# A fused two-layer kernel on one core: the first two weight units of layer 1 are fetched together and run chunk by chunk

## The chip, the cores and the metric

One Trainium2 chip, one of its cores. The metric is the device time of one execution in microseconds (us); where several executions are given, it is their median. The engines are PE (TensorE, matmuls), DVE (VectorE), ACT (ScalarE), POOL (GpSimd) and SP (SyncE, which here only issues DMA). ACT and POOL issue DMAs of their own as well.

## What is computed

Two layers over 1024 latent tokens and 256 context tokens, model width 1024, batch 1, all in float32. Layer 0 mixes tokens by two chunkwise recurrences, layer 1 by windowed attention and by a diagonal state-space scan (S5). The reference, cut to the second layer:

```python
h = rmsnorm(x, norm_g[layer]) * (1 + scale) + shift          # for latents and for context
q, k, v, g_att, u, g_s5 = split_cols(h @ w_in, OD_SPLITS)    # widths 1024, 256, 256, 1024, 1024, 1024
att = window_attention(rope(q), rope(k), v, sink)            # 128-token band, all context keys, a sink
ssm = s5_bidirectional(u, ...)                               # 64 groups of 16 channels, 64 complex states each
z = gelu(ssm); a, b = split(z @ glu_w, 2); s5 = a * sigmoid(b)
y = concat([att * silu(g_att), s5 * silu(g_s5)]) @ w_out
out = rmsnorm(x + gate * y, final_norm_g)                    # latents only
```

## The kernel before

**Matmuls of float32 in three passes.** A weight unit is a tile of 128 x 1024: 128 output features by 8 blocks of 128 inputs. SP loads it (`wraw`, line 116, one buffer), ACT rounds it to its high part `whi` (line 64) and DVE subtracts to get the low part `wlo` (line 65). The token side is held the same way as `hh` and `hl`. `mm3` (lines 69 to 71) then runs three matmuls for each block: high by high, high by low, low by high. A chunk of tokens costs 8 x 3 = 24 matmuls into one PSUM tile named `mm`, of which there are two.

**Chunks.** The tokens lie in three chunks, `CHUNKS`: 256 context tokens (`hh0`, `hl0`), then 512 latents (`hh1`, `hl1`), then the last 512 (`hh2`, `hl2`). The normalised rows of the last chunk are the last thing that layer 0's output stage makes: PE transposes them (line 287), DVE scales them (`nt`, line 294), ACT and DVE split them into `hh2` and `hl2` (lines 64 and 65).

**Weight stream.** `Stream` hands units out in a fixed order. `get` cuts the next unit (splits it into `whi` and `wlo`) if that is not done yet and issues the next load; `ahead` cuts the unit after that while the current one runs. In layer 1 the even units among the first ten live in one pool, `pre`, and the odd ones in another, one buffer for each half. `g_fm` runs one unit over all its chunks: get, then for each chunk 24 matmuls, the evacuation, and `ahead(0)` after the first chunk.

**Layer 1** (`layer1`) weaves two threads in program order. `main()` runs the layer's products, called *layer matmuls* here: eight `u` units (evacuated by `ev_u` to `sg`, line 949, and sent to DRAM as `uF` from ACT's DMA queue, line 950), then `v`, two `k` units, and the units of gates and `q`. `side()` runs S5 on 32 pairs of channel groups, called *pairs 0 to 31*. For a pair, the *front* is a product on PE (`pd<-ut,bt`, line 1611), its copy on ACT (`sd`, lines 1615 to 1617), the scan with its multiplications on DVE (`rq` and `uw`, lines 1628 to 1638) and a copy on ACT (`sx`, lines 1640 and 1641). The *back* is products on PE into `yo` (line 1651 with `mt`, line 1653 with `sx`). For every second pair a set of matrices is built on PE, ACT, DVE and through small SP transfers (`s5kd`, `mt`, lines 1542 and 1545). Pair 4k needs the u units up to k, which `nu` counts.

**Order.** The kernel is built with a scheduler of the tile framework (`schedule_with_timeline_sim=True`): it takes the program order, the dependences and the buffers and fixes one order for every engine, which then runs in that order. So an edit at the start of layer 1 can change rows much later. Layer 0 and everything up to the transposes of the last chunk stand in the same order on PE in both kernels. After layer 1's weave, attention, the GLU products and the output products follow.

Of the kernel before, what the change touches and what calls it, by code (L numbers as in the profile page):

```python
# [54 lines left out]
class Body:  # L55
# [92 lines left out]
    def g_fm(self, st, hs, evac):  # L148

        (wh, wl), = st.get()  # L150
        for ci, (hh, hl, c0, n) in enumerate(hs):
            ps = self.bank("mm", 2)
            for ko in range(8):
                w = slice(ko * 128, ko * 128 + 128)
                self.mm3(ps[:, :n], wh[:, w], wl[:, w], hh[:, ko, :], hl[:, ko, :], ko == 0, ko == 7)
            evac(ps[:, :n], c0, n)
            if ci < st.hl_b - 1:
                st.ahead(ci)
            yield

    def g_tm(self, st, hs, evac):
# [742 lines left out]
    def layer1(self):  # L904
# [13 lines left out]
        st = self.st  # L918
# [9 lines left out]
        with tc.tile_pool(name="psum1", bufs=1, space=PSUM, reuse_waits="tile") as ps5:  # L928
            s5 = S5(self, ps5, uF, zF)
            nu = [0]  # L930
# [12 lines left out]
                    yield  # L943

            def main():
                for i in range(8):
                    def ev_u(ps, c0, n):
                        t = self.stg.tile([128, 512], F32, name="sg", tag="sg", bufs=2)[:, :n].rearrange("p (t n) -> p t n", t=8)
                        S.activation(t, ps.rearrange("p (n t) -> p t n", t=8), AF.Copy)
                        self.nc.scalar.dma_start(  # L950
                            uF[i * 8:i * 8 + 8, :, c0 // 8:(c0 + n) // 8].rearrange("g (h t) n -> (g h) t n", t=8), t)

                    yield from self.g_fm(st, self.hs, ev_u)
                    nu[0] += 1

                def ev_v(ps, b):
# [17 lines left out]
                for kind, i in oB:  # L974
                    def ev(ps, c0, n):
                        lc = slice(c0 - 256, c0 - 256 + n)
                        if kind == "q":
                            self.rope(ps, c0, n, 0.125, [
                                qD[lc.start // 128:lc.stop // 128, i // 2, a * 32:a * 32 + 32,
                                   i % 2 * 2 + h].rearrange("b d t -> d b t")  # L980
                                for a in range(2) for h in range(2)])
                        elif kind == "ga":
                            t = self.silu(ps, n)
                            self.nc.scalar.dma_start(gaD[i, :, lc], t)
                        else:
                            t = self.stg.tile([128, 8, 64], F32, name="sg", tag="sg", bufs=2)
                            S.activation(t, ps.rearrange("p (n t) -> p t n", t=8)[:, ::-1], AF.Silu)
                            self.nc.scalar.dma_start(gsD[i, :, :, lc.start // 8:lc.stop // 8], t)

                    yield from self.g_fm(st, self.hs[1:], ev)  # L990

            weave(main(), side(), 24 + 10 + 6 + 2 * len(oB) - 6, s5.steps + 9)
        self.right.close()
        if self.stop == "l1":
# [4 lines left out]
        with ExitStack() as low:  # L999
# [23 lines left out]

            att = self.g_att(ai, ap, pa, qD, kD, vD, gaD)
            main = main()
            advance(main)
            advance(att)
            weave(main, att, 46, 150)
# [774 lines left out]
```

## Time and profile before

| | us |
|---|---|
| median of 3 runs | 2721.9 (2720.25 to 2723.5) |
| the profiled execution | 2724.01 |
| its span in the trace | 2722.2 |
| layer 1's layer matmuls and S5, about | 1551 to 2150 |
| attention, GLU and output products | from about 2150 to the end |

The trace covers 2722.2 us of the profiled execution's 2724.01; the other 1.8 us lie around it, and its mean granted clock was 0.99. The profiled execution is 2.1 us above the median of the runs. All positions below are microseconds from the span's start. PE records of float32 products that are not split (those of S5) appear twice for each instruction, so that four products show as x8.

### The profile page before, as it was taken

The page shows a single profiled execution, that of the slowest core. Times are in us where ns is not written, and L with a number is a line of the kernel's source. Part 1 is how long each engine was busy: PE and PEld are TensorE (multiplying, and loading weights), DVE is VectorE, ACT ScalarE, POOL GpSimd, SP SyncE. Part 2 cuts the span into 40 slices and gives each one's busy share as a digit, 9 for nine tenths or more (in the row PEclk, how much of TensorE's full clock was granted, in tenths as well). Part 3 has the DMA queues.
Part 4 walks back from the last instruction along what each step waited for, and adds up shares of the span by engine and source line. Part 5 has one row for each costly group of instructions (what it writes and reads, how often), then busy time and mean ns, then how long its engine had stood idle before and what let it go on. Part 6 is the DMA issues. An engine that isn't in the chain of part 4 may idle for free. (4 is left out here: it accounts for less than half of the span.)

```text
span 2722.2 us, 44690 instructions
## 1 busy us (share of the span) xinstructions
PE 2636.9 (97%) x15680; PEld 2274.3 (84%) x15680; DVE 1861.4 (68%) x4794; ACT 1374.3 (50%) x2917; POOL 488.4 (18%) x881
## 2 busy tenths in 40 slices
PE   6999999999999999999999999899999999999998
PEld 3998989898798898888787788787888888888887
DVE  5556655464664565646657688899994488898896
ACT  5445545434545445436324324677775455576552
POOL 1121121212212222222100000010010022225520
PEclk9999999999999999999999999999999999999999
DMA  6001011111111111112454545345446523253333
GB/s 243 28 31 56 21 57 35 49 53 53 57 49 47 57 57 32 57 57 84 142 187 146 177 122 137 93 118 127 118 109 182 157 83 112 78 159 112 124 115 130
DMA packets 235520, 262.15 MB, mean 96 GB/s; under 512 B 87520, under 2 KB 179936, under 8 KB 235040
## 3 DMA queue, kind: packets, MB, share of 16 engines
q1 hardware_dynamic: 174528, 223.89, 26.9%
q10 hardware_dynamic: 55712, 20.46, 2.9%
q0 software_dynamic: 5056, 14.95, 1.8%
q8 instruction: 124, 2.03, 0.3%
q14 instruction: 100, 0.82, 0.1%
HBM read 192.69 MB, written 66.52 MB: 95 GB/s over the span
## 5 line engine op out<-in xcount | busy, mean ns | idle before, releaser
L69 PE MATMUL mm<-hh,whi 128*128 128x512 f32 (+1 forms) x1800 | 671.4, 373 | 15.3 <-ACT gt L583 5.1
L71 PE MATMUL mm<-hh,wlo 128*128 128x512 f32 (+1 forms) x1800 | 668.0, 372 | 0.9 <-DVE wlo L65 0.8
L70 PE MATMUL mm<-hl,whi 128*128 128x512 f32 (+1 forms) x1800 | 663.6, 369 | 0.5 <-DVE hl L65 0.5
L69 PEld LDWEIGHTS mm<-hh,whi 128*128 128x128 f32 x1800 | 340.9, 189 | 69.5 <-issue 6.6
L71 PEld LDWEIGHTS mm<-hh,wlo 128*128 128x128 f32 x1800 | 340.1, 189 | 55.6 <-issue 1.8
L70 PEld LDWEIGHTS mm<-hl,whi 128*128 128x128 f32 x1800 | 340.6, 189 | 52.9 <-DVE hl L65 1.2
L70 PE MATMUL mm<-owl,yh 128*128 128x512 f32 x576 | 226.2, 394 | 4.8 <-DVE owl L65 4.7
L69 PE MATMUL mm<-owh,yh 128*128 128x512 f32 x576 | 226.8, 395 | 1.4 <-ACT yh L64 1.4
L71 PE MATMUL mm<-owh,yl 128*128 128x512 f32 x576 | 226.3, 394 | 0.0
L65 DVE TENSOR_TENSOR wlo<-wraw,whi 128x1024 fp32r<-128x1024 f32 x117 | 145.3, 1242 | 95.7 <-ACT whi L64 95.3
L69 PE MATMUL mm<-whi,hh 128*128 128x256 f32 x720 | 205.7, 286 | 3.1 <-DVE v L364 3.1
L70 PE MATMUL mm<-wlo,hh 128*128 128x256 f32 x720 | 205.4, 285 | 0.0
L71 PE MATMUL mm<-whi,hl 128*128 128x256 f32 x720 | 202.5, 281 | 0.0
L64 ACT ACTIVATE whi<-wraw 128x1024 fp32r<-128x1024 f32 x117 | 123.6, 1056 | 125.7 <-PE mm L70 104.9
L563 DVE SCALAR_TENSOR_TENSOR S<-S,sc,st 128x128 f32<-128x128 f32 (+1 forms) x192 | 74.3, 387 | 161.8 <-PE st L558 161.3
L1155 ACT ACTIVATE P<-P,ast 128x640 f32<-128x640 f32 (+1 forms) x128 | 101.6, 796 | 99.8 <-DVE ast L1156 66.7
L1161 POOL TENSOR_TENSOR P<-P,ast 128x640 f32<-128x640 f32 (+1 forms) x64 | 87.1, 1361 | 342.5 <-DVE ast L1159 199.2
L69 PEld LDWEIGHTS mm<-whi,hh 128*128 128x128 f32 x720 | 135.6, 188 | 5.1 <-DVE v L364 4.1
L70 PEld LDWEIGHTS mm<-wlo,hh 128*128 128x128 f32 x720 | 136.0, 189 | 1.4 <-issue 0.2
L71 PEld LDWEIGHTS mm<-whi,hl 128*128 128x128 f32 x720 | 135.5, 188 | 0.6
L70 PEld LDWEIGHTS mm<-owl,yh 128*128 128x128 f32 x576 | 108.3, 188 | 28.2 <-DVE owl L65 7.2
L69 PEld LDWEIGHTS mm<-owh,yh 128*128 128x128 f32 x576 | 108.2, 188 | 26.2 <-ACT ot L870 3.4
(407 smaller groups left out, 6071.5 us busy)
## 6 DMA issues: line engine op xcount, KB each, us to landing
wraw<-in_w SPq DMA_DIRECT2D x117, 512.0 KB, 3.7
yr<-yT SPq DMA_DIRECT2D x144, 128.0 KB, 2.6
owr<-in_wo SPq DMA_DIRECT2D x62, 256.0 KB, 5.5
whi<-in_wada SPq DMA_DIRECT2D x24, 512.0 KB, 3.5
adaw<-in_adaw SPq DMA_DIRECT2D x16, 512.0 KB, 10.2
qr<-qD SPq DMA_DIRECT2D x64, 128.0 KB, 2.8
yT<-gt SPq DMA_DIRECT2D x28, 256.0 KB, 2.3
x1p<-xr SPq DMA_DIRECT2D x10, 512.0 KB, 3.5
```

Of the source, the lines that this page charges most:

```text
L64: self.S.activation(hi, src, AF.Copy)
L65: (eng or self.V).tensor_tensor(lo, src, hi.bitcast(F32), op=OP.subtract)
L69: T.matmul(ps, sh, mh, start=first, stop=False)
L70: T.matmul(ps, sh, ml, start=False, stop=False)
L71: T.matmul(ps, sl, mh, start=False, stop=last)
L563: V.scalar_tensor_tensor(new, state[d], scal(d, b, 6, 7), pst[:, :dv], op0=OP.mult, op1=OP.add)
L1155: S.activation(p[:, j, :w], p[:, j, :w], AF.Exp, bias=nm[:, j:j + 1], accum_out=sm[:, j:j + 1])
L1161: G.tensor_tensor(p[:, 1, :w], p[:, 1, :w], es[:, 1:2].to_broadcast([128, w]), op=OP.mult)
```

## The change

The generator `fm` is new: `g_fm` without its own `get` and `ahead`. The first two u units are taken by one `get(2)`. Four runs of `fm` follow: unit 0 over the chunks 0 and 1, unit 1 over the chunks 0 and 1, unit 0 over chunk 2, unit 1 over chunk 2. `ahead(0)`, which cuts unit 2, comes after unit 0's chunk 2, and each of the two units is counted in `nu` after its chunk 2. The six other u units go through `g_fm` as before. `ev_u` becomes a factory, so that it keeps the unit's number. Lines of the changed kernel are 9 higher from line 160 on and 20 higher behind this place.

```diff
--- before.py
+++ after.py
@@ -156,6 +156,15 @@
             evac(ps[:, :n], c0, n)
             if ci < st.hl_b - 1:
                 st.ahead(ci)
+            yield
+
+    def fm(self, wh, wl, hs, evac):
+        for hh, hl, c0, n in hs:
+            ps = self.bank("mm", 2)
+            for ko in range(8):
+                w = slice(ko * 128, ko * 128 + 128)
+                self.mm3(ps[:, :n], wh[:, w], wl[:, w], hh[:, ko, :], hl[:, ko, :], ko == 0, ko == 7)
+            evac(ps[:, :n], c0, n)
             yield
 
     def g_tm(self, st, hs, evac):
@@ -943,14 +952,25 @@
                     yield
 
             def main():
-                for i in range(8):
-                    def ev_u(ps, c0, n):
+                def ev_u(i):
+                    def ev(ps, c0, n):
                         t = self.stg.tile([128, 512], F32, name="sg", tag="sg", bufs=2)[:, :n].rearrange("p (t n) -> p t n", t=8)
                         S.activation(t, ps.rearrange("p (n t) -> p t n", t=8), AF.Copy)
                         self.nc.scalar.dma_start(
                             uF[i * 8:i * 8 + 8, :, c0 // 8:(c0 + n) // 8].rearrange("g (h t) n -> (g h) t n", t=8), t)
 
-                    yield from self.g_fm(st, self.hs, ev_u)
+                    return ev
+
+
+                us = st.get(2)
+                for k, hs in ((0, self.hs[:2]), (1, self.hs[:2]), (0, self.hs[2:]), (1, self.hs[2:])):
+                    yield from self.fm(*us[k], hs, ev_u(k))
+                    if hs[0] is self.hs[2]:
+                        nu[0] += 1
+                        if k == 0:
+                            st.ahead(0)
+                for i in range(2, 8):
+                    yield from self.g_fm(st, self.hs, ev_u(i))
                     nu[0] += 1
 
                 def ev_v(ps, b):
```

ACT at the start of layer 1, before, with what each row waits for. `nt` is the scaled last chunk, `sg` a unit's evacuation (`mm_16989` and `mm_17124` are unit 0's chunks 0 and 1), `whi_17017` unit 1's high part:

```order
L64 ACTIVATE hh2_15700<-nt_16958 128x2x256 [waits DVE_49]
L949 ACTIVATE sg_17014<-mm_16989 128x256 [waits DMAHW0_49,PE_49]
L64 ACTIVATE whi_17017<-wraw_16559 128x1024
L949 ACTIVATE sg_17149<-mm_17124 128x512 [waits DMAHW7_49,DMAHW1_49,PE_49]
L950 DMA uF_16970<-sg_17014 1024x1x32 [waits DMAHW4_49,Activation_49]
```

The same place after. Unit 1's high part is now `whi_16989`, unit 0's chunk 0 is `mm_16995`:

```order
L64 ACTIVATE hh2_15700<-nt_16958 128x2x256 [waits DVE_49]
L64 ACTIVATE whi_16989<-wraw_16559 128x1024
L958 ACTIVATE sg_17020<-mm_16995 128x256 [waits DMAHW0_49,PE_49]
L958 ACTIVATE sg_17149<-mm_17124 128x512 [waits DMAHW7_49,DMAHW1_49,PE_49]
L959 DMA uF_16970<-sg_17020 1024x1x32 [waits DMAHW6_49,Activation_49]
```

Unit 1's split changes places with the first evacuation, and both still stand behind the last split of `hh2`. On PE the products of unit 1 over chunks 0 and 1 stand behind the last transposes in the place where unit 0's chunk 2 stood.

PE in the S5 pairs, before: `yo_20010` and `yo_20160` are the back products of pairs 14 and 15, `sb` and `sk` build matrices, `pd` is a front product, and `mm_20678` and `mm_20715` are layer matmuls (the rows left out between two `mm` rows are of the same two tiles):

```order
L1653 MATMUL yo_20010<-sx_19670,ct_19565 128x128 x2
L70 MATMUL mm_20678<-hl2_15701,whi_20466 128x512
...
L1514 MATMUL sb_20043<-cst_63,G_20031 128x128 x4
L1520 MATMUL sk_20049<-G_20031,kc_20027 32x128 x8
L1611 MATMUL pd_20064<-ut_19913,bt_19705 128x160 x4
L1651 MATMUL yo_20160<-ut_19606,mt_19556 128x128
L71 MATMUL mm_20678<-hh2_15700,wlo_20467 128x512
...
L71 MATMUL mm_20715<-hh1_15698,wlo_20602 128x512
L1653 MATMUL yo_20160<-sx_19823,ct_19565 128x128 x2
```

The same place after, without a row left out:

```order
L1673 MATMUL yo_20010<-sx_19670,ct_19565 128x128 x2
L1671 MATMUL yo_20160<-ut_19606,mt_19556 128x128
L1534 MATMUL sb_20037<-cst_63,G_20031 128x128 x4
L1534 MATMUL sb_20043<-cst_63,G_20031 128x128 x4
L1540 MATMUL sk_20049<-G_20031,kc_20027 32x128 x8
L1631 MATMUL pd_19922<-ut_19913,bt_19705 128x160 x4
L1673 MATMUL yo_20160<-sx_19823,ct_19565 128x128 x2
L1671 MATMUL yo_20160<-ut_19606,mt_19556 128x128
L1673 MATMUL yo_20160<-sx_19823,ct_19565 128x128 x2
L1544 MATMUL sk_20049<-cst_63,kq_20058 128x128
L69 MATMUL mm_20430<-hh1_15698,whi_20315 128x512
```

After pair 12's back products no layer matmul stands on PE until behind pair 15's; the next one is `mm_20430`, whose weights are the unit `whi_20315`.

SP at the load of that unit, `wraw_20158`, before (`bq`, `kc`, `dd` are constants of S5, `s5kd` and `mt` the small transfers of its matrices, `ut` reads `uF`):

```order
L116 DMA wraw_20008<-in_w1 128x1024
L1542 DMA s5kd_70<-kfb_19132 16x4x16 x8
L1545 DMA mt_19250<-s5kd_70 16x4x128 x8
L1504 DMA kc_20027<-in_s5kc 128x256
L116 DMA wraw_20158<-in_w1 128x1024
```

And after:

```order
L1562 DMA s5kd_70<-kfb_19730 16x4x16 x8
L1624 DMA ut_19913<-uF_16970 16x4x160 x2
L1565 DMA mt_19864<-s5kd_70 16x4x128 x8
L1624 DMA ut_19913<-uF_16970 16x4x160
L116 DMA wraw_20158<-in_w1 128x1024
```

The load moved behind the transfers of two further sets of matrices (`mt_19556` and `mt_19864`).

## Rows read from the trace of the kernel before

**Rows 1.** The page's busy times.

```profile
PE 2636.9 (97%) x15680; PEld 2274.3 (84%) x15680; DVE 1861.4 (68%) x4794; ACT 1374.3 (50%) x2917; POOL 488.4 (18%) x881
```

**Rows 2.** Timeline, PE, start of layer 1: start, us, engine, line, tiles, idle before.

```profile
1562.65 0.63 PE L287 MATMUL o<-cst,xn 128*128 128x128 f32 x4 [0.86 <-DVE nt L294]
1563.56 0.63 PE L287 MATMUL o<-cst,xn 128*128 128x128 f32 x4 [0.28 <-DVE nt L294]
1567.80 0.79 PE L69 MATMUL mm<-hh,whi 128*128 128x512 f32 x1 [3.62 <-ACT sg L949]
...
1571.38 0.63 PE L71 MATMUL mm<-hh,wlo 128*128 128x512 f32 x1
1571.81 0.57 PE L69 MATMUL mm<-hh,whi 128*128 128x512 f32 x1
...
1572.45 0.40 PE L71 MATMUL mm<-hh,wlo 128*128 128x512 f32 x1
1572.68 0.39 PE L69 MATMUL mm<-hh,whi 128*128 128x512 f32 x1
```

**Rows 3.** Busy by stretch, PE alone: length, busy (records), PEclk, DMA share, GB/s.

```profile
1567.80:1571.80 4.00, 4.00 (x9) 0.50 0.50 95
```

**Rows 4.** Timeline, ACT, the same place.

```profile
1566.85 0.63 ACT L64 ACTIVATE hh<-nt 128x512 fp32r<-128x512 f32 x1 [1.07 <-DVE nt L294]
1567.38 0.37 ACT L949 ACTIVATE sg<-mm 128x256 f32<-128x256 f32 x1
1567.65 1.05 ACT L64 ACTIVATE whi<-wraw 128x1024 fp32r<-128x1024 f32 x1
1568.60 0.58 ACT L949 ACTIVATE sg<-mm 128x512 f32<-128x512 f32 x1
```

**Rows 5.** Waits of PE, 1740 to 1910: us in total, times, longest.

```profile
PE yo L1653 <- ACT sx L1641: 9.8, 3, 8.5
```

**Rows 6.** Timeline, PE: front of pair 4, backs of pairs 4, 12 and 15.

```profile
1731.46 1.25 PE L1611 MATMUL pd<-ut,bt 128*128 128x160 f32 x8
1732.55 0.33 PE L1537 MATMUL sk<-kfb,shift 128*128 128x64 f32 x2
...
1744.63 1.22 PE L1653 MATMUL yo<-sx,ct 128*128 128x128 f32 x4 [8.53 <-ACT sx L1641]
...
1844.28 0.61 PE L1653 MATMUL yo<-sx,ct 128*128 128x128 f32 x4
...
1879.67 0.61 PE L1653 MATMUL yo<-sx,ct 128*128 128x128 f32 x4
```

**Rows 7.** Timeline, ACT: the last copy before pair 15's back.

```profile
1875.32 0.63 ACT L1641 ACTIVATE sx<-uw 64x512 f32<-64x512 f32 x1
```

**Rows 8.** Timeline, DVE, behind it: a low part and a rotary step.

```profile
1878.73 1.22 DVE L65 TENSOR_TENSOR wlo<-wraw,whi 128x1024 fp32r<-128x1024 f32 x1 [0.29 <-ACT whi L64]
1879.87 1.48 DVE L1632 TENSOR_TENSOR_SCAN rq<-dec,sd 128x640 f32<-128x640 f32 x1
...
1889.01 0.69 DVE L897 TENSOR_TENSOR rp<-mm,rot 128x512 f32<-128x512 f32 x1 [1.26 <-ACT rp L895]
1889.62 0.68 DVE L898 TENSOR_TENSOR rp<-rp,rot 128x512 f32<-128x512 f32 x1
```

**Rows 9.** Busy by stretch: length, PE, PEld, DVE, ACT, POOL (records), PEclk, DMA.

```profile
1844.30:1879.70 35.40, 31.84 (x198) 26.65 (x197) 35.01 (x49) 24.94 (x50) 0.00 (x0) 0.95 0.47 118
1879.70:2068.30 188.60, 187.19 (x1064) 157.94 (x1063) 178.50 (x249) 137.24 (x249) 16.67 (x32) 1.00 0.48 118
2068.30:2300.00 231.70, 231.70 (x1247) 199.92 (x1246) 148.62 (x383) 117.33 (x231) 34.78 (x35) 1.00 0.47 136
```

**Rows 10.** The same view, attention and output stages to the end.

```profile
2300.00:2450.00 150.00, 145.96 (x868) 127.80 (x867) 130.06 (x385) 94.21 (x222) 33.72 (x28) 0.98 0.38 118
2450.00:2600.00 150.00, 147.45 (x881) 129.80 (x880) 130.79 (x360) 91.79 (x230) 76.01 (x59) 1.00 0.40 126
2600.00:2722.00 122.00, 109.28 (x559) 93.12 (x557) 95.22 (x286) 47.63 (x114) 17.05 (x14) 0.96 0.34 113
```

## Prediction

> **What bounds the kernel now.** I read the page's busy shares first, then PE's waits and idle gaps in layer 1, then the timelines of the engines around the gaps, and last the busy times by stretch. The reader is to see that PE is busy 97% of the span, far ahead of DVE's 68% and ACT's 50% [rows 1]. So a change is worth what it does to PE's idle time and to its clock, and nothing else.
>
> Two places in layer 1 have idle time that this change can touch. The first is the hole that the change aims at. PE's last transposes of chunk 2 end at 1564.19, and unit 0's chunk 2 starts at 1567.80 after 3.62 us of idle [rows 2]. With the two short gaps between the transposes (0.86 and 0.28 [rows 2]) that is 4.8 us. Behind it PE runs at a granted clock of 0.50, the 1.2 GHz level [rows 3]. The 512-wide matmuls start 0.43 us apart there, and 0.23 apart from 1572.4 on [rows 2]; some ten starts at 0.2 us too much make 2.0 us. The second place is the S5 pairs, where PE waits 9.8 us in all for `sx`, 8.5 of them at pair 4 [rows 5, 6].
>
> In the S5 pairs the reader is to see two engines close to full at once. From pair 12's back to pair 15's DVE is busy 35.01 of 35.40 us while PE is busy 31.84; from there to pair 31's back PE is busy 187.19 of 188.60 and DVE 178.50; then PE has no idle time for 231.7 us [rows 9]. So around pairs 12 to 15 DVE sets the pace and layer matmuls fill PE's time under it. Afterwards PE sets it.
>
> **The hole: filled or not.** The new order puts 48 matmuls of unit 1 behind the transposes: 24 of the width 256 and 24 of 512, ready except for unit 1's weights and the PSUM tiles. But the order of ACT decides. Unit 1's split stands behind the last `hh2` split there, which ends at 1567.48 [rows 4]. The evacuation that frees PE's first tile now follows the split instead of going ahead of it. Split 1.05 and evacuation 0.37 [rows 4] end at 1567.48 + 1.05 + 0.37 = 1568.9, where before the evacuation ended at 1567.75 and PE went on at 1567.80 [rows 2, 4]. So I take the hole to be 1.0 us longer, not shorter. The bounds are 0, if the evacuation's end overlaps as it does now, and 2, since the second tile and `wlo` come later still. The fall of the clock stays and costs what it cost. Had the hole been filled, it would be worth at most 4.8 + 2.0 = 6.8 us. Unit 2's split waits for unit 0's chunk 2 now, since both use `pre`; it is hidden by unit 1's chunk 2, 24 matmuls at 0.23 = 5.5 us against a split of 1.05 and a low part of 1.22 [rows 4, 8].
>
> **Pair 4.** In the new order pair 4's front product stands behind 7 matmuls of a chunk where it stood behind 16. Nine matmuls at 0.23 are 2.1 us. ACT and DVE had idle time there, so `sx` comes 2.1 to 2.5 us earlier, and the 8.5 us wait shrinks by as much: I take 2.3. From here to pair 15 DVE sets the pace, so this is carried by DVE.
>
> **Pairs 12 to 15.** This is the large term. A weight load moved back on SP behind the transfers of two further sets of matrices, and the scheduler set PE's order by it. I counted, in both orders, what stands ahead of pair 15's back product. 108 layer matmuls that stood ahead of it stand behind it now, and with them 4 front products. At 0.23 us [rows 2] the matmuls are 24.8 us; 4 front products take 1732.55 - 1731.46 = 1.1 us [rows 6]. So PE owes 25.9 us more at this point.
>
> What it gets for that is an earlier start of pair 15's back, and three things limit it. DVE's work ahead of this pair is smaller by what belongs to the moved matmuls, counted in DVE's order: 3 low parts at 1879.87 - 1878.73 = 1.14 and 6 rotary steps at 0.61 [rows 8], 7.1 us in all. PE is late for this pair today: `sx` ends at 1875.95 and the back starts at 1879.67 [rows 6, 7], so 3.7 us. And DVE is 2.3 - 1.0 = 1.3 us ahead from pair 4 and the start. That makes 12.1 us earlier, at 1867.6. PE's extra debt is therefore 25.9 - 12.1 = 13.8 us. The waits that show it are at the backs of pairs 13, 14 and 15, where PE has 6.3 us, 1.5 us and 5.0 us of work ahead of them by the order and DVE needs about 11 us for each pair (35.4 us for three, [rows 9]).
>
> **Does the debt stay?** Behind pair 15 PE has 187.2 + 25.9 = 213.1 us of work up to pair 31, and DVE 178.5 + 7.1 = 185.6 [rows 9]. PE is the longer by 27 us, so it isn't starved again and the debt isn't hidden. In the 231.7 us behind that there is no idle time to take it up either [rows 9]. The same work follows to the end. From about 2420 on the rows of PE are woven anew; the idle time from 2300 to 2722 is 4.0 + 2.6 + 12.7 = 19.3 us [rows 10], and I can't price how much of it changes: 0, with 3 us to both sides.
>
> **The sum.** +1.0 (hole) and -2.3 (pair 4) are inside the 13.8. The profiled execution would go from 2724.0 to 2737.8, and the median, which lies 2.1 below it, from 2721.9 to 2735.7, so **2736**. Its own range is the bounds: 1 us at the hole, 3 us for DVE's pace (the step from pair to pair isn't even), 3 us at the end, and upward 2 us if the late weight load or a fall of the clock behind the last of the new waits is on the path: 2730 to 2742.
>
> **Rivals.**
>
> *The change does what it says* (faster). Its place is ACT at 1567, its price 6.8 us, plus the 2.3 us of pair 4: 2721.9 - 9.1 = 2713. It decides only if unit 1's split runs ahead of the `hh2` splits, in the time that ACT is idle before them, and if the layer matmuls at pairs 12 to 15 aren't missed. The order of the rows speaks against both. I leave 8%.
>
> *PE makes up its debt* (no change). Weight loads keep PEld busy 157.94 of 188.60 us from pair 15 to 31, 84%, and 199.92 of 231.70 behind [rows 9]. If matmuls could close up to that, there would be 30 us of room behind pair 15 and the 13.8 us would vanish, so 2721.9 + 1.0 - 2.3 = 2721. Against it: the 512-wide starts are 0.23 apart wherever PE waits for nothing, and a stretch of 231.7 us without a gap shows no closer ones. The Trainium skill, "Perfetto Trace Analysis", section "Identifying the Most-Contended Engine", says that matmul busy time is no good measure for how near PE is to its limit, and that the busy share of weight loads is better; by that rule this rival would hold, and the trace doesn't bear it out here. To this I add the case that the end, woven anew, gives back 9 us or more of its 19.3 [rows 10], which also lands near 2725. Together 24%.
>
> *The new waits cost the clock too* (slower still). PE dropped to half its clock behind a wait of 3.62 us [rows 2, 3], which cost 2.0. If it does so behind three new waits, and the work behind each is on the path, that is 6 us; if the late load also holds up the first matmuls behind pair 15 by its way through ACT and DVE (1.05 + 1.22, [rows 4, 8]) and some SP transfers, 4 more: 2736 + 10 = 2746. The Trainium skill, "TensorE: Matmul & The Clock Gate", section "Why this matters for your kernels", says that idle gaps between bursts of matmuls bring the clock back to half; the rows agree. While DVE sets the pace a slow PE loses nothing, so only the last of the three should count. 16%.
>
> **How the numbers follow.** Forecast 52%, rivals 8, 24 and 16%. The range is to leave out no more than 2 in 10: I drop the faster rival (8%) and the outer half of the last one (some 8%), which gives 2719 to 2748. A measurement of this kernel can tell about 0.2%, 5.4 us, from no change. Slower by more than that holds the forecast and the last rival, 0.68; within it the second rival, 0.24; faster the first, 0.08.
>
> **What would show it.** In the changed kernel's profile: PE's gap behind the last transposes 4 to 5 us long, ended by an ACT row, with a clock of 0.50 behind it (right), or gone (wrong). The wait at pair 4 near 6 us. Waits of PE for `sx` at the backs of pairs 13, 14 and 15 of some 4 to 9 us each, 15 to 22 us in all, where before the two besides pair 4's make 1.3 us together [rows 5]. Pair 15's back near 1868, pair 31's near 2082 where it was at 2068. DVE busy the same from pair 12 to 15. If pair 31's back is at or before 2068, the large term is wrong; if it is at 2082 and the time is still 2722, the end took it back; if the waits are there and the back of pair 15 is later than 1872, DVE's pace is the step that I mis-sized.

## The result, and the profile after

The changed kernel takes 2749.99 us (median of 4 runs, 2748.26 to 2752.22) where the kernel before takes 2721.79 (4 runs): a ratio of 1.0103, with an interval of 1.009 to 1.0115. It is slower, as forecast, but by 28.2 us instead of 14, and 2 us outside the range. The profiled executions differ by 25.8 us (2749.76 against 2724.01). The other 2.4 us are the place of the two profiled executions among their runs: before's was 2.2 above its median, after's is 0.2 below. The positions below belong to the profiled executions.

The page's busy times of after, against [rows 1]:

```profile
PE 2646.2 (96%) x15680; PEld 2281.3 (83%) x15680; DVE 1867.6 (68%) x4794; ACT 1371.7 (50%) x2914; POOL 487.0 (18%) x881
```

PE's busy time is 9.3 us longer and its span 25.8, so PE is idle for 16.5 us more, with the same 15680 records. That allows a plain measure of where time is lost: the start of the n-th record of PE after, less the start of the n-th before. I call it the *delay* at record n. It is -0.2 at record 9200 (1552 us in before, ahead of anything that the change touches), 0.8 at 10200 (1717 us in before), -2.2 at 10600, 11.6 at 11000 (1869, pair 15), 16.0 at 12200 (2082, behind the pairs), 16.0 at each hundred up to 13800 (2371), then 17.3 at 14600, 21.1 at 15000, 22.1 at 15400 and 25.8 at the last. So there are two losses, 16.0 at the pairs and 9.8 from attention on, with some 290 us between them in which nothing changes.

The start of layer 1 (timeline of PE and a stretch of it, against [rows 2, 3]; the columns of a stretch are start and end, length, busy time of PE, PEld, DVE, ACT and POOL with records, PEclk, DMA share, GB/s):

```profile
1563.27 0.63 PE L296 MATMUL o<-cst,xn 128*128 128x128 f32 x4 [0.28 <-DVE nt L303]
1568.46 0.58 PE L69 MATMUL mm<-hh,whi 128*128 128x256 f32 x1 [4.56 <-ACT sg L958]
...
1568.46:1572.46 4.00, 4.00 (x18) 3.81 (x19) 3.62 (x17) 0.43 (x1) 0.00 (x0) 0.55 0.67 108
```

The hole is 4.56 where it was 3.62, still ended by the evacuation `sg`, with a granted clock of 0.55 behind it: the 1.2 GHz level for most of these 4 us.

The pairs (timeline of PE, backs of pairs 4 and 13 to 15, against [rows 6]; then PE's waits from 1740 to 1910, against [rows 5]):

```profile
1742.54 1.23 PE L1673 MATMUL yo<-sx,ct 128*128 128x128 f32 x4 [5.98 <-ACT sx L1661]
...
1853.21 1.22 PE L1673 MATMUL yo<-sx,ct 128*128 128x128 f32 x4 [3.37 <-ACT sx L1661]
...
1859.51 1.23 PE L1673 MATMUL yo<-sx,ct 128*128 128x128 f32 x4 [2.28 <-ACT sx L1661]
...
1866.24 1.97 PE L1534 MATMUL sb<-cst,G 128*128 128x128 f32 x8 [2.96 <-DVE G L1583]
1870.49 0.71 PE L1673 MATMUL yo<-sx,ct 128*128 128x128 f32 x4
```

```profile
PE yo L1673 <- ACT sx L1661: 12.1, 4, 6.0
PE sb L1534 <- DVE G L1583: 3.2, 2, 3.0
PE sk L1557 <- DVE kfb L1548: 1.8, 1, 1.8
```

Busy by stretch, the stages of [rows 9], then the whole of [rows 10] in one row for after and one for before:

```profile
1843.00:1870.50 27.50, 16.76 (x113) 13.93 (x111) 27.35 (x40) 17.21 (x38) 0.00 (x0) 0.69 0.37 90
1870.50:2083.10 212.60, 211.70 (x1176) 178.76 (x1177) 190.39 (x261) 145.80 (x264) 16.67 (x32) 1.00 0.47 116
2083.10:2314.90 231.80, 231.80 (x1246) 199.93 (x1246) 148.36 (x381) 116.95 (x232) 34.40 (x35) 1.00 0.48 138
...
2316.00:2748.00 432.00, 407.33 (x2304) 352.31 (x2302) 359.70 (x1026) 234.26 (x563) 125.23 (x101) 0.97 0.37 117
```

```profile
2300.00:2722.00 422.00, 402.69 (x2304) 350.71 (x2302) 356.07 (x1026) 233.62 (x563) 126.77 (x101) 0.98 0.37 119
```

The reader is to see: from pair 12's back to pair 15's PE is busy 16.76 of 27.50 us at a mean granted clock of 0.69, with DVE full; from pair 15 to 31 PE is full for 212.6 us instead of 188.6; then full for 231.8, as it was for 231.7; and the last stage has the same 2304 records in 432.0 instead of 422.0 us. Of these 10.0 us, 5.4 are idle time of PE (24.7 against 19.3) and 4.6 are longer busy time at a granted clock of 0.97 instead of 0.98. Two rows of the last stage in after end waits of over 2 us (before has one there, of 3.0 us). The first is in attention: `sc` are its scores, `ast` the maxima that DVE takes of earlier scores. The second is in the output products: `ot` is a finished product that DVE takes out of the PSUM tile `mm`. Behind each stands the stretch of 4.7 us from there, in which the clock is 0.64 and 0.50 (timeline of PE, busy by stretch):

```profile
2595.79 0.45 PE L1161 MATMUL sc<-kh,qa 128*128 128x384 f32 x1 [2.29 <-DVE ast L1157]
2595.79:2600.49 4.70, 4.70 (x17) 3.98 (x18) 3.64 (x13) 3.11 (x9) 1.25 (x1) 0.64 0.87 243
...
2713.32 0.76 PE L69 MATMUL mm<-owh,yh 128*128 128x512 f32 x1 [4.05 <-DVE ot L881]
2713.30:2718.00 4.70, 4.68 (x11) 3.73 (x12) 4.55 (x20) 1.89 (x5) 0.00 (x0) 0.50 0.62 215
```

### The profile page after: what moved, and what is told of

Same layout as the page of the kernel before. It is cut to its first block, busy times and chain, and to the rows that moved or that the text cites. A ratio compares the mean times of both kernels' runs of the same rounds, so it can differ in the third digit from the quotient of the medians.

```text
span 2748.0 us, 44673 instructions
## 1 busy us (share of the span) xinstructions
PE 2646.2 (96%) x15680; PEld 2281.3 (83%) x15680; DVE 1867.6 (68%) x4794; ACT 1371.7 (50%) x2914; POOL 487.0 (18%) x881
## 3 DMA queue, kind: packets, MB, share of 16 engines
q1 hardware_dynamic: 174528, 223.89, 26.8%
## 4 chain that ended last, share of the span: by engine, by line
PE 78%; DVE 10%; ACT 6%; DMA 4%; issue 2%; SPq 1%; ACTq 0%; POOL 0%; DVEq 0%; POOLq 0%
PE mm L69 19%; PE mm L71 19%; PE mm L70 19%; PE o L556 3%; PE pt L1192 2%; PE st L567 2%; PE att L527 2%; DVE tmp L457 2%; PE pv L1200 1%; PE pv L1201 1%; PE sc L1162 1%; PE sc L1161 1%; ACT L408 1%; PE pd L1631 1%; PE att L528 1%
```

## The experiments

Many of them take the order of one program's rows and lay it on another: the program is built once to read each engine's order, and a second time with this order as dependences inside each engine that add no wait. "single" is the program text of before, "pair" that of after, `rows` the order, `FREE` the instructions of the first two u units. A range behind a ratio is its 95% interval. The delay is against the profiled execution of before. Executions differ by up to 3 us in layer 0, where all kernels are the same: the delay at record 9200 is 2.1 in one run here and -3.0 in another. A delay called *net* is less that of record 9200.

### The first two units alone, the pairs alone, the end alone

```diff
-    nc, _ = build(arrays, "pair")
+    _, rows = build(arrays, "single")
+    nc, _ = build(arrays, "pair", rows, lambda eng, k: k not in FREE)
```

> The changed first two units, but every other instruction of the program is held, on each engine, in the order of the kernel before (by issue-order edges without a wait). Theory A (the new order of the rest is the cost): only the start of layer 1 is left, where the trace of the changed kernel shows PE's hole 0.94 us longer, so 2721.8 + 0.7 = 2722.5, within 2721 to 2725; the pairs end at 2068 to 2070. Theory B (the units themselves cost: inputs of S5 later, clock): above 2735, the pairs end at 2080 or later.

Measured: 2723.90 against 2720.48, 1.001 (1.0001 to 1.0019). The net delay is 0.3 at record 9400, behind the hole (4.57 us long), 1.8 behind the pairs and 0.6 at the end. So what the diff writes costs some 0.1%; the other nine tenths of the loss come from the order of the rest.

```diff
+    _, old = build(arrays, "single")
+    _, new = build(arrays, "pair")
+    rows = splice(old, new, {"PE": (0, 11000), "Activation": (0, 2200), "DVE": (0, 3600), "SP": (0, 1000), "Pool": (0, 500)})
+    nc, _ = build(arrays, "single", rows, lambda eng, k: k not in FREE)
```

This has before's units and after's order up to attention (PE's instruction 11000 lies in it), and before's order from there. The next one has the ranges turned round, `(11000, None)` and so on: after's order from attention on alone.

> The units of the kernel before; from there through the S5 pairs every engine is held in the order of the changed kernel, and from attention on in the order of the kernel before. Theory A: the pairs end 15 to 16 us later than before and the end keeps its length, so 2721.8 + 15.3 = 2737, within 2734 to 2740. Theory B: near 2722 to 2726. If the end of the kernel takes the delay back, the pairs end late and the time is still below 2730.

> The units and the pairs of the kernel before; from the middle of attention on every engine is held in the order of the changed kernel. Theory A (the end woven anew costs by its own order): 2721.8 + 9.8 = 2731.6, within 2729 to 2735. Rival (the extra 9.8 us at the end come from arriving there late, with other transfers in flight): 2720 to 2725.

Measured: 2738.61, 1.0059 (1.0042 to 1.0076), with a net delay of 17.7 behind the pairs and 19.1 at the end; and 2732.72, 1.0045 (1.003 to 1.006), with -0.7 up to record 13800, 4.2 at 15000 and 8.6 at the end. The two losses add up: 17.7 at the pairs and 9.3 from there to the end (8.6 + 0.7) make 27.0, where after has 26.0 net. PE's waits in the last stage of the second:

```profile
PE sc L1175 <- DVE ast L1171: 5.3, 8, 2.3
PE mm L70 <- DVE ot L882: 3.8, 1, 3.8
```

The wait for `ot` is what after shows at its end and before doesn't; the waits for `ast` make 5.0 us in after and 3.1 before.

### Is it SP's order

SP's rows alone are put into before's order, so that the late weight load goes ahead again:

```diff
-    nc, _ = build(arrays, "pair")
+    _, rows = build(arrays, "single")
+    nc, _ = build(arrays, "pair", rows, lambda eng, k: eng == "SP" and k not in FREE)
```

> The changed kernel, in which SP alone is held in the order of the kernel before (outside the first two units); the scheduler orders the other engines anew. Theory C (the weight load's later place on SP is what let PE run out of layer matmuls): PE's order then has 29 layer matmuls more ahead of pair 15's back than before instead of 108 fewer, PE waits less than 5 us for sx at the backs of pairs 12 to 17, and the pairs end at 2064 to 2072. Rival (the scarce stretch comes from elsewhere, DVE's pace or the transfers themselves): the pairs end at 2078 or later. The time at the end can't be told, since the end is woven anew: 2715 to 2735 under theory C.

Measured: 2729.89, 1.0035 (1.0022 to 1.0048). As expected, 29 more layer matmuls stand ahead of pair 15's back than in before, where after has 108 fewer. But that back stands at 1888.6, later than in either kernel, pair 31's is at 2083.3, after's place, and the net delay behind the pairs is 10.0. SP's late load is not the whole cause: the scheduler wove yet another order around it.

### A new weave with nothing moved

The two units are fetched together, and the chunks run in before's order:

```diff
+                us = st.get(2)
+                for k in range(2):
+                    for hs in (self.hs[:1], self.hs[1:2], self.hs[2:]):
+                        yield from self.fm(*us[k], hs, ev_u(k))
+                        if k and hs[0] is self.hs[0]:
+                            st.ahead(0)
+                    nu[0] += 1
```

> Before's kernel with one half of the change: the two units' weights are asked for together, but the chunks run in the old order, unit 0 over all three and then unit 1 over all three; the rest is put into order anew, so that 60 layer matmuls fewer stand ahead of pair 15's back than before (1200 for 1260; after has 108 fewer). Theory A (what costs is the order that the rest falls into, whatever the two units do): slower than before although no chunk has moved, pairs' end 5 to 10 us later than before's, 2725 to 2740 in all. Theory B2 (the cost comes with the chunk order, and with after's own order alone): within 0.2% of before, 2717 to 2726.

Measured: 2742.63, 1.0075 (1.006 to 1.009), slower as expected and 2.6 us above the range. The net delay is 8.8 behind the pairs and 17.2 at the end, with the waits for `ot` (3.8) and `ast` (6.2) again. Not one chunk was moved here. Fetching and splitting unit 1 one step earlier is enough to make the scheduler weave the rest anew, and both new weaves lose at the same two stages.

### Is it DVE's pace

In the prediction DVE sets the pace around pairs 12 to 15. Its three rows a pair that make the table `tb` are moved to POOL, with every order otherwise kept, in before and in after:

```diff
-        V = self.V
+        V = self.nc.gpsimd
         r, u = (self.wt("tb", (128, 2, 160), 2) for _ in range(2))
```

> Before, every engine's order as it was, with the three small table steps of each pair (tb, 1.27 us of VectorE's time a pair) on GpSimd, which is 8% busy there. Theory D (VectorE's rows set the pace of pairs 12 to 15): VectorE has up to 14 us less to do over pairs 4 to 15, of which before can use little, since PE is 96 to 99% busy there: pairs' end 2 to 8 us earlier, 2713 to 2721. Theory R (VectorE doesn't set the pace, PE's own order does): within 2 us, 2719 to 2724. If GpSimd is late with the tables, or its work slows VectorE's, slower: over 2725.

> After, every engine's order as it is, with the same table steps on GpSimd. Theory D: after's pairs 12 to 15 waited for VectorE and PE could use what VectorE is relieved of; the pairs end 2070 to 2076 instead of 2083.1, and the distance to the same kernel with before's order shrinks from 16 us to 4 to 11; 2736 to 2743 in all. Theory R: the distance stays at 14 to 18 us and the time within 3 us of 2750. With a late GpSimd: over 2753.

Measured: 2729.52, 1.0028 (1.0018 to 1.0037), and 2758.33, 1.0136 (1.0121 to 1.0151). Both are slower, as the third case of the expectations has it, and DVE won nothing. Groups of rows from 1750 to 2050 (form, count, busy time, mean ns): one of POOL and two of DVE with the tables on POOL, then the same two and the table's row of before.

```profile
L1610 POOL TENSOR_SCALAR tb<-tb 128x320 f32<-128x320 f32 x24 | 47.6, 1985 | 2.0
...
L1667 DVE TENSOR_TENSOR_SCAN rq<-dec,sd 128x640 f32<-128x640 f32 x24 | 38.0, 1583 | 0.2
L1598 DVE TENSOR_TENSOR ct<-ct,Gu 128x1024 f32<-128x1024 f32 x12 | 17.1, 1425 | 0.0
```

```profile
L1632 DVE TENSOR_TENSOR_SCAN rq<-dec,sd 128x640 f32<-128x640 f32 x24 | 35.6, 1484 | 0.0
L1563 DVE TENSOR_TENSOR ct<-ct,Gu 128x1024 f32<-128x1024 f32 x12 | 14.6, 1218 | 0.0
L1575 DVE TENSOR_SCALAR tb<-tb 128x320 f32<-128x320 f32 x24 | 7.7, 320 | 0.0
```

The row takes 1985 ns on POOL and 320 on DVE, and meanwhile the two rows of DVE are 7% and 17% longer. So this pair doesn't test the theory. The next pair does: the table's rows are left out for all pairs but the first.

```diff
+        if p and self.K.one_table:
+            self.tabs[p] = self.tab0
+            return
         r, u = (self.wt("tb", (128, 2, 160), 2) for _ in range(2))
```

> Before, every engine's order as it was, with the table rows (tb, 1.27 us of VectorE's time a pair) done for pair 0 alone and its table used for all pairs, so that the output is another. Theory D (VectorE's rows set the pace of the pairs): before can use only what PE waits there, at most 4 to 6 us over pairs 4 to 31, so the pairs end 2062 to 2068 instead of 2068.3 and the kernel takes 2714 to 2721. Theory R (PE's own order sets it): within 2 us, 2719 to 2724.

> After, every engine's order as it is, with the table rows of pair 0 alone as in the kernel beside it (the output is another). Theory D: after's pairs 12 to 15 wait for VectorE, which has 1.27 us less to do in each, some 14 us over pairs 4 to 15; the pairs end 2070 to 2077 instead of 2083.1, and the distance to the kernel beside it with before's order falls from 14.8 to 5 to 11 us; 2736 to 2744 in all. Theory R: the distance stays at 13 to 18 us.

Measured: 2721.28, 0.9998 (0.9989 to 1.0008), and 2749.01, 1.0097 (1.0082 to 1.0112). The net delay behind the pairs is -2.5 and 18.1 (after 16.2). With some 30 us of DVE's work gone from 1750 to 2050 (of the three rows the one shown above is 7.7 us), before gains 2.5 us at the pairs and nothing that the medians show, and after nothing at all: the distance between the two orders grows to 20.6 us, where the theory of DVE's pace wanted 5 to 11. In after the work became waiting: DVE's wait from 1700 to 1950, and a stretch from pair 13 to 20, without the table's rows and then in after:

```profile
DVE G L1596 <- PE sk L1555: 10.2, 3, 6.6
```

```profile
1850.00:1950.00 100.00, 88.84 (x506) 74.25 (x507) 91.30 (x115) 72.87 (x138) 8.34 (x16) 0.91 0.47 117
...
1850.00:1950.00 100.00, 89.77 (x511) 75.32 (x512) 98.48 (x137) 73.47 (x140) 8.33 (x16) 0.91 0.48 117
```

DVE is busy 91.30 instead of 98.48 here, and PE still only 88.84. A full DVE was not what held PE, and the theory of DVE's pace falls. What is left is the chain of hand-overs between PE, ACT and DVE for each pair; that is argued, and no run shortened it.

### Can the holes be filled

After's holes at pairs 13 to 15 are filled by hand: the late load goes ahead again on SP, its split on ACT and DVE, and 48 layer matmuls on PE, all other rows as in after.

```diff
+    a, b = products(rows, "PE", (20430, 20519))
+    ahead(rows, "SP", ["I-20159"], "I-19607")
+    ahead(rows, "Activation", ["I-20317"], "I-20402")
+    ahead(rows, "DVE", ["I-20318"], "I-19704")
+    ahead(rows, "PE", a[:16], "I-19833")
+    ahead(rows, "PE", a[16:] + b[:8], "I-20012")
+    ahead(rows, "PE", b[8:], "I-20038")
```

> After; only one unit's weights and products are moved: their load from the 1866.8th us on SP to the 1836th, their two splits from the 1871st and 1873rd to the 1842nd and 1843rd, and their first 48 products from behind pair 15's back into PE's holes: 16 ahead of pair 13's back, 16 ahead of pair 14's, 16 ahead of the sb transposes (48 by 0.23 us are 11 us of PE). Theory H (the 16 us come from PE's order: nothing stood in the waits of the pairs' chain, since the next unit's weights came late on SP): PE's waits for sx and G there go, pair 15's back stays within 3 us of 1870.6, the pairs end 8 to 12 us earlier (2071 to 2075 instead of 2083.1) and the kernel takes 2738 to 2743. Theory K (the pairs' chain through VectorE and ScalarE sets the end of the pairs, whatever PE does meanwhile): pairs' end within 3 us of 2083, 2747 to 2751.

Measured: 2751.04, 1.0109 (1.0092 to 1.0126): no gain. The stretches from pair 12 to 15 and from there to pair 16, and the second again of after:

```profile
1840.40:1870.80 30.40, 24.95 (x160) 20.43 (x158) 29.29 (x42) 17.94 (x38) 0.00 (x0) 0.94 0.32 79
1870.80:1889.10 18.30, 9.58 (x57) 7.81 (x57) 17.29 (x23) 12.89 (x23) 4.16 (x8) 0.81 0.40 96
```

```profile
1870.50:1889.00 18.50, 17.65 (x106) 14.60 (x107) 17.50 (x21) 14.15 (x24) 4.17 (x8) 1.00 0.46 110
```

The holes are filled (24.95 us busy where after had 16.76 of 27.50), and the same time is missing behind pair 15: 9.58 busy of 18.30 where after has 17.65 of 18.50. Pair 16's back stands at 1889.16, after's at 1888.96, before's at 1890.33: pair 16 comes no earlier with PE's holes ahead of it filled. Counted from layer 1's start (-3.0 and -0.2 in the table below) it comes some 3 us later, and net the delay behind the pairs is 20.6 instead of 16.2.

The same on before, for the 8.53 us of pair 4 [rows 6]: 48 matmuls go ahead of its back.

```diff
+    a, b = products(rows, "PE", (19624, 19733))
+    ahead(rows, "SP", ["I-19414"], "I-18370")
+    ahead(rows, "Activation", ["I-19448"], "I-19510")
+    ahead(rows, "DVE", ["I-19449"], "I-18361")
+    ahead(rows, "PE", a + b, "I-18485")
```

> Before; one unit's weights are asked for 23 us earlier on SP, split in the idle times of ScalarE and VectorE near 1729 and 1731, and its first 48 products (24 of 256 columns, 24 of 512: 8.3 us of PE) stand ahead of pair 4's back, where PE waits 8.53 us. Theory M (PE's idle time counts wherever it lies, as theory H says of pairs 13 to 15): PE is 7 to 9 us ahead behind pair 4, most of it stays to the end, 2712 to 2716, better than both kernels. Theory L (VectorE is 98 to 99% busy from pair 5 to 19, so PE's lead turns into waits for sx): the pairs end within 4 us of 2068.3, 2718 to 2723.

Measured: 2722.06, 1.0001 (0.9991 to 1.001). Filled, then before:

```profile
1733.50:1743.70 10.20, 10.00 (x60) 8.65 (x59) 9.63 (x15) 7.01 (x12) 0.00 (x0) 1.00 0.27 64
1743.70:1770.20 26.50, 18.66 (x111) 15.76 (x110) 26.46 (x35) 16.14 (x34) 0.00 (x0) 0.86 0.34 91
```

```profile
1734.00:1744.60 10.60, 2.11 (x13) 1.68 (x11) 9.78 (x14) 7.22 (x13) 0.00 (x0) 0.76 0.31 69
1744.60:1772.40 27.80, 26.05 (x159) 22.57 (x159) 27.77 (x37) 17.89 (x36) 0.00 (x0) 0.91 0.38 106
```

The hole is gone, and PE is busy 7.4 us less behind it. The net delay behind the pairs is 0.6. Neither of the holes that were filled had a price of its own.

### More filler ahead

If a missing filler is paid later, filler added ahead should pay. The weave's count for the layer thread is raised by 6 and by 12 in before; the scheduler orders the rest.

```diff
-            weave(main(), side(), 24 + 10 + 6 + 2 * len(oB) - 6, s5.steps + 9)
+            weave(main(), side(), 24 + 10 + 6 + 2 * len(oB) - 6 + (6), s5.steps + 9)
```

> Before with one number of the weave changed: 6 more layer steps are reckoned with, so that from pair 17 on more layer products are laid ahead of the pairs (56 more ahead of pair 25's back, 131 more ahead of pair 31's), order made anew. Theory N (the accounting: behind pair 25 PE is full, so the delay at the start of attention is pair 25's delay less 0.226 us for each product laid ahead of it): if the added products fill PE's idle time (some 7 us between 1750 and 2050) pair 25 is 6 to 13 us later and the delay behind the pairs is -7 to 0 us; with an end of 0 to +5: 2715 to 2727. Whatever pair 25's delay, the delay behind the pairs should be that less 12.7 us, to 0.5 us. Theory O (the accounting holds by chance for this change): the two differ by over 2 us.

> The same with 12 more steps: 176 more products ahead of pair 25's back, 254 more ahead of pair 31's. Theory N: pair 25 some 33 to 40 us later, the delay behind the pairs that less 39.8 us (to 1 us), -7 to 0 us; since only the last pairs run behind the last of the layer products now, PE may wait for them: up to +10 more. 2715 to 2735 in all. Theory O: no such relation.

Measured: 2736.66, 1.0052 (1.0035 to 1.0069), and 2759.52, 1.0135 (1.0118 to 1.0152); both ranges were missed. At pair 25's back 56 and 176 more matmuls are done than in before, and the back is 11.6 and 38.4 us later, net. At 0.226 us each (the distance of 512-wide starts) the matmuls are 12.7 and 39.8 us: what is added ahead delays the pair by nearly its own time and wins 1.1 to 1.4 us. Behind the pairs more than that is lost, since the layer's matmuls are used up and nothing fills PE there. From 2050 to 2150, where before's PE had no idle time from 2068 on [rows 9]: with 12, then with 6.

```profile
2050.00:2150.00 100.00, 80.59 (x404) 66.29 (x402) 46.57 (x56) 45.54 (x72) 8.34 (x16) 0.91 0.48 131
```

```profile
2050.00:2150.00 100.00, 96.44 (x447) 78.77 (x446) 42.62 (x51) 47.86 (x66) 8.33 (x16) 0.98 0.66 178
```

And both, woven anew, lose 8 to 10 us more from record 13000 to the end (delays of 2.2 and 10.1, 22.3 and 32.6).

### The end

The wait for `ot` could come from late loads of `xr`, the rows that the products are added to, or from DVE's order. First the loads: the last rows get buffers of their own, so that SP asks for them 10 to 20 us earlier.

```diff
-            x = wp.tile([128, 1024], F32, name="xr", tag="xr", bufs=xb)
+            own = xpool and self.rows_own and b - b0 >= 4
+            x = (xpool if own else wp).tile([128, 1024], F32, name="xr", tag="xr", bufs=xb)
```

> After, every engine's order as it is, but the input rows of the last four output blocks have buffers of their own and are asked for ahead of the first two stores of the output on SP instead of behind them. Theory E (the end's 9.8 us come from these loads landing late: VectorE waits, PE waits 4.0 us for the bank and then runs at half clock): PE's 4.0 us wait for ot goes, the clock stays at 1.0 in the last 60 us, 2742 to 2746. Theory F (they come from the output products standing later against the attention's last block, so that little PE work is left to hide the last block's norms and stores): the wait for ot is replaced by another, within 2 us of after, 2748 to 2752.

Measured: 2750.21, 1.0105 (1.009 to 1.012), and the wait is 6.22 us instead of 4.05. The run is not a clean test, since the early loads brought a wait of their own. ACT now waits for a later load, `yr`, of which it makes `yh`, and DVE behind ACT (timelines of ACT and DVE; after has neither wait at this place):

```profile
2704.94 0.42 ACT L66 ACTIVATE yh<-yr 128x256 fp32r<-128x256 f32 x1 [2.93 <-DMA yr<-yT]
2705.39 0.43 DVE L67 TENSOR_TENSOR yl<-yr,yh 128x256 fp32r<-128x256 f32 x1 [3.08 <-ACT yh L66]
```

What speaks against the loads is after's own row: ahead of the wait's end DVE waits 0.51 us for `xr`, and is busy otherwise. DVE's timeline there:

```profile
2708.13 1.28 DVE L1061 SCALAR_TENSOR_TENSOR xr<-xr,rs,fg 128x1024 f32<-128x1024 f32 x1
2709.53 1.09 DVE L65 TENSOR_TENSOR yl<-yr,yh 128x256 fp32r<-128x256 f32 x3
...
2711.21 1.29 DVE L882 TENSOR_TENSOR xr<-xr,ot 128x512 f32<-128x512 f32 x2 [0.51 <-DMA xr<-x2p]
2712.49 1.28 DVE L881 TENSOR_TENSOR ot<-mm,gbl 128x512 f32<-128x512 f32 x2
```

Norm rows of finished blocks (line 1061) stand ahead of `ot`, which frees PE's tile. So the evacuations go ahead of the norm rows on DVE, with the loads that they need on SP and the buffers of the run before:

```diff
+    for eng, names, ahead in (("DVE", (29501, 29529, 29594), 29264), ("DVE", (29622, 29595, 29623), 29655),
+                              ("SP", (29379, 29473), 29649), ("SP", (29567,), 29265), ("SP", (29661,), 29657)):
```

> After, order of PE, ScalarE and GpSimd as it is. At the very end VectorE takes block 5's two products out of their banks (ot, with the sums of block 4 and 5) ahead of the norms of blocks 2 and 3 instead of behind them, and the last four blocks' input rows have buffers of their own and are asked for ahead of the first two output stores. Theory G (PE's 4.0 us wait for ot comes from some 9 us of norm rows that stand ahead of ot on VectorE): the wait falls to under 1 us, the clock stays at 1.0 up to 2720, and the kernel ends 4 to 7 us earlier, 2743 to 2746. Theory F2 (the norms have to be done by the end in any case, and the last block's chain sets it): the wait goes but comes back behind it, 2748 to 2752.

Measured: 2744.85, 1.0087 (1.007 to 1.0104), 5.1 us less than after by the medians and 4.4 by the delay. PE's row behind the shorter wait, and the 4.7 us behind it:

```profile
2722.30 0.47 PE L71 MATMUL mm<-owh,yh 128*128 128x512 f32 x1 [2.24 <-DVE ot L884]
...
2722.30:2727.00 4.70, 4.70 (x21) 3.88 (x22) 3.13 (x11) 1.15 (x2) 0.00 (x0) 1.00 0.28 112
```

The wait is 1.8 us shorter, though not under 1 us as expected, and the clock stays at 1.00, where after did 11 products in the time of 21, at 0.50. The Trainium skill, "TensorE: Matmul & The Clock Gate", section "Why this matters for your kernels", says that idle gaps between bursts of matmuls bring the clock back to half; the row behind after's 4.05 us agrees. A wait's length alone does not tell here whether the clock falls: behind 2.24 us it stayed, and behind 2.29 us in after's attention it fell.

Both edits together, the holes and the end:

> The kernel beside it with the end's change of e13_after_evacuations_first as well. If the two causes are separate stretches and PE is the bound behind both, the gains add: 5 us less than the kernel beside it, 2733 to 2738. If the end's wait goes with the earlier pairs already: within 2 us of the kernel beside it.

Measured: 2749.46, 1.0101 (1.0086 to 1.0116), 1.6 us below the holes alone, not 5. The wait is 1.89 us here, and was 3.85 with the holes alone. PE's row behind the wait and the 4.7 us behind it, then these of the holes alone:

```profile
2724.19 0.46 PE L71 MATMUL mm<-owh,yh 128*128 128x512 f32 x1 [1.89 <-DVE ot L884]
2724.19:2728.89 4.70, 4.70 (x14) 3.71 (x15) 3.13 (x11) 1.15 (x2) 0.00 (x0) 0.64 0.28 112
...
2714.96:2719.66 4.70, 4.70 (x14) 3.72 (x15) 4.47 (x19) 1.88 (x5) 0.00 (x0) 0.64 0.61 218
```

The wait is 2.0 us shorter, but the clock fell behind it all the same, to 0.64 in both kernels. The loss from record 13800 to the end is 1.9 us smaller (8.6 to 6.7), as the wait is; with the evacuations alone it was 4.4 smaller (9.8 to 5.4), since there the clock stayed as well.

## Why the prediction was right and wrong

**The sum behind the pairs held, partly by luck.** Predicted 13.8, measured 16.0. Of its steps, the 108 moved matmuls and the 25.9 us were right by the order, and the gain that pair 15's back gets for them was mis-sized: 12.1 predicted, 1879.67 - 1870.49 = 9.2 measured [rows 6]. 25.9 - 9.2 = 16.7, of which 0.7 came back. Pair 31's back was to be at 2082 and stands at 2083.02, where before's is at 2068.32.

The reason given for it did not hold, and that is the luck. The prediction had DVE set the pace, and took 7.1 us of DVE work off pair 15. Without the table's rows the place of pair 15 gains nothing (1871.20, after 1870.49). What the runs show instead is a ledger. From pair 25's back to record 13000, behind the pairs, PE has no idle time in before and after. So the delay there is that back's delay plus 0.226 us for each layer matmul that is still missing ahead of it (negative where more of them are done there than in before):

| kernel | layer 1's start | pair 25's back | matmuls missing | sum | behind the pairs | net |
|---|---|---|---|---|---|---|
| after | -0.2 | 1.3 | 64 | 15.8 | 16.0 | 16.2 |
| units alone | 2.1 | 3.9 | 0 | 3.9 | 3.9 | 1.8 |
| pairs alone | -1.2 | 1.8 | 64 | 16.3 | 16.5 | 17.7 |
| SP's order of before | 0.5 | 13.3 | -13 | 10.4 | 10.5 | 10.0 |
| new weave, nothing moved | -2.1 | -2.5 | 40 | 6.5 | 6.7 | 8.8 |
| before, tables on POOL | -0.2 | 7.1 | 0 | 7.1 | 7.1 | 7.3 |
| after, tables on POOL | -1.9 | 10.1 | 64 | 24.6 | 26.8 | 28.7 |
| before, one table | -1.1 | -3.6 | 0 | -3.6 | -3.6 | -2.5 |
| after, one table | -0.7 | 2.7 | 64 | 17.2 | 17.4 | 18.1 |
| after, holes filled | -3.0 | 2.9 | 64 | 17.4 | 17.6 | 20.6 |
| before, hole filled | -1.4 | -0.8 | 0 | -0.8 | -0.8 | 0.6 |
| before, weave + 6 | -2.9 | 8.7 | -56 | -4.0 | 2.2 | 5.1 |
| before, weave + 12 | -2.6 | 35.8 | -176 | -4.0 | 22.3 | 24.9 |

It is bookkeeping and no mechanism: it says that pair 25's back hardly moves (2005.98 before, 1.3 later after) while 64 matmuls less fit ahead of it. The holes are where this is seen, not what it costs; two runs filled them for nothing. The last two rows are where it ends, and by the measure on record for these two runs (0.5 and 1 us) it fails there: the delay is 6.2 and 26.3 us above the sum. With more matmuls ahead than the layer can spare, PE is idle for 3.6 and 25.0 us between pair 25's back and record 13000, and the clock falls. Why after's order fits 64 less in the same time is not settled beyond this: it is not SP's late load alone, not DVE's busy time and not the holes at pairs 13 to 15.

**The waits were placed wrong.** Predicted for `sx` at the backs of 13, 14 and 15: 15 to 22 us. Measured: 3.37, 2.28 and none. The rest of PE's 10.7 idle us lies at other hand-overs (`sb` 2.96), and its busy time is stretched by a mean clock of 0.69, 0.95 before [rows 9].

**The hole and pair 4 were right.** 4.56 us, ended by ACT, with the clock low behind it (predicted 4.6, 4 to 5); 5.98 at pair 4 (predicted near 6).

**The debt stayed.** The delay is 16.0 at record 12200 and 16.0 at 13800. The rival that PE makes it up fell: with PEld busy 199.93 of 231.80 us, 86%, PE made up nothing. By the rule of the Trainium skill, "Perfetto Trace Analysis", section "Identifying the Most-Contended Engine", 14% would be room; the trace does not agree for these matmuls.

**The end is the step that failed:** "0, with 3 us to both sides" was 9.8 in the delay. The prediction saw that the rows are woven anew there and could not price it, and set bounds narrower than the 19.3 us at stake. It also counted idle time alone, where 4.6 of the 10.0 us are a lower clock. After's order alone, laid on before's start, brings 9.3 of it. Some 4 to 5 us of it hang on one place of DVE's order in the last 40 us, norm rows ahead of `ot`, with the clock that this costs. Of the 3.8 us that attention's second half loses between records 14600 and 15000, 1.6 are more idle time of PE, by the wait of 2.29 us for `ast` shown above, and behind that wait the clock falls. Why `ast` comes late is open: no run took it apart.

The rival "the new waits cost the clock too", with 2746, came nearest in size, but for a place that lost little: the clock was low at the pairs, and filling the holes there brought it to 0.94 and gained nothing. The waits that cost the clock and the time stood in the last stage. A second raw-weight buffer, which would free the late load without any new order, was not tried. No version here beats before.

## What to carry to other kernels

Where a scheduler fixes the order of the whole program, price an edit by the whole order that it makes: a fetch and a split moved by one step cost 0.75% here, far from the edit. Between two interleaved threads, count how much filler is done by the last slot that waits for the other thread, because the two holes that were filled locally only moved, and filler used up early was missing behind. Read the last 50 us row by row: there little is left to hide a wait behind.

## What the runs showed of the hardware

A three-row table build moved to GpSimd took 1.2 to 2.0 us a row instead of 0.3 to 0.5, and meanwhile VectorE's own rows with two inputs in SBUF became 2 to 29% longer, the two rows shown 7% and 17%. A row that takes one input from PSUM (`mm`) did not become longer, 676 instead of 684 ns (groups from 1750 to 2050, with the tables on POOL, then before):

```profile
L908 DVE TENSOR_TENSOR rp<-mm,rot 128x512 f32<-128x512 f32 x16 | 10.8, 676 | 1.4 <-ACT rp L906 1.4
...
L897 DVE TENSOR_TENSOR rp<-mm,rot 128x512 f32<-128x512 f32 x18 | 12.3, 684 | 2.1 <-ACT rp L895 2.1
```

The Trainium skill, "GPSIMD Engine Reference", section "Specifications", says that the two share their SBUF interfaces and contend when a VectorE instruction has two SBUF inputs, and the rows agree: both of the longer rows shown have two. Moving the table between these two engines was no free trade here, although GpSimd was 8% busy.
